# A block substitution in a two-layer mixer kernel: three runs of 128 blocks on GpSimd instead of four of 96 on two engines

## The chip, the core and the metric

The kernel runs on one core of a Trainium2 chip. The core has TensorE (PE, with its weight loads shown as PEld), VectorE (DVE), ScalarE (ACT), GpSimd (POOL) and SyncE (SP), which here issues every DMA. Each engine, and SP's queue of DMAs, executes its instructions in the order in which they stand in the program; between engines semaphores order the work. The metric is device time in microseconds (us) of one execution, as the median of several runs.

## The reference

Two blocks are computed one after the other for 512 tokens of width 2048, in fp32. The first has a state-space mixer (SSD) and a gated delta rule mixer (GDN) side by side, the second a layer with HGRN2 and an RG-LRU and a layer with an mLSTM. The change lies in the GDN of the first block: 8 heads, 2 directions, 6 chunks of 128 tokens (2 of context, 4 of latents). Cut to what matters:

```
gcum = cumsum(g);  decay = exp(where(incl, gcum[i] - gcum[j], -inf))
a_strict = where(strict, (k*beta) @ k.T * decay, 0)              # 128 x 128 for each head, direction, chunk
sol = triangular_solve(a_strict, rhs, left_side=True, lower=True, unit_diagonal=True)
u, w = sol[..., :V], sol[..., V:]
# then over the chunks:  v_new = u - w @ S;  o = q_dec @ S + attn @ v_new;  S = S*dec + k_end.T @ v_new
```

The kernel does the triangular solve by inverting (I + a_strict): first the 32 x 32 blocks on the diagonal, by substitution, and from these the inverse of 64 x 64 and of 128 x 128 with matmuls. There are 8 heads x 2 directions x 6 chunks x 4 blocks = 384 such 32 x 32 blocks.

## The kernel before

Every large matrix product multiplies fp32 weights that are split into a high and a low part of type fp32r. `gemm_steps` streams them: a DMA `wr` (L182) brings four blocks of 128 x 128, ScalarE copies them to `wh` (L185), VectorE makes the rest `wl` (L186), and TensorE does three products for each (L200). There are 4 buffers of `wr` and 6 of `wh` and `wl`.

**Phase A** (`phase_a`, some 0 to 705 us) projects and convolves. Its last part makes, head by head, what the recurrence needs: `gdn_prep(h)` loads `kf`, `vf`, and decay rows `E`; on GpSimd stand L677 (six subtractions on `E`), L703 (a square root of six columns, for which L702 on VectorE must be done) and L684 (a mask). It ends with L742, which stores the head's 48 diagonal blocks in DRAM, in `LX`. Between the heads stand the projections of the later heads' keys and values. In this phase a scheduler decides the order of all engines.

**The substitution** is `gdn_solve`: a DMA brings blocks from `LX`, one block per partition, into `T` (L751); GpSimd writes the diagonal (L753); then come 31 steps of a product (L758, `To<-T`) and a subtraction (L760, `T<-T,To`), 62 instructions of 31 to 256 elements per partition, each of which needs the one before it; GpSimd masks the result (L761) and writes the diagonal (L763), and a DMA stores it in `LT` (L764). It is called four times for two heads (96 blocks) each: twice in phase A with GpSimd as its engine, twice in phase B with VectorE.

**Phase B** (`phase_b`, some 700 to 1115 us) runs the recurrence of the 8 heads. `gdn_load(h)` (loads at L961: `X`, and `ZF`, `WB` from `LT`) and GpSimd's L902 and L905 prepare the inverse, `gdn_merge` builds it (matmuls `mg`, L928), `gdn_ctx` and `gdn_lat` walk over the chunks: `ks` (L975), `rS` on VectorE (L976), `vn` (L983), and so on. In `gdn_lat` the norm of q is made as `rq`: ScalarE writes it (L1033), GpSimd raises it in place to the power -1/2 (L1034), VectorE scales it in place (L1067); the scaled value is used only at the head's end (L1072). Between these small matmuls TensorE works through the projections of `z` and the later queries; `ssd_gate` adds up squares on GpSimd (L1190), and after four of them `ssd_norm` sums over partitions with the matmul `rs` (L294). In phase B TensorE's order is that of the code, written by hand (`weave`, `feed`); the scheduler orders the other engines and SP.

After it come the output projection, the gate and the second block; nothing there is touched.

Of the kernel before, what the change touches and what calls it, by code (L numbers as in the profile page):

```python
# [15 lines left out]
P = 128  # L16
# [117 lines left out]
class Prog:  # L134
# [606 lines left out]
                x = xt  # L741
            nc.sync.dma_start(self.LX[h, d].rearrange("c b r n -> (b r) c n"), x)  # L742

    def gdn_solve(self, h, g, eng):

        nc = self.nc
        n = 96
        flat = lambda t: t[h:h + 2].rearrange("a d c b r n -> (a d c b) (r n)")
        T = g.tile([n, 32, 32], F32, name="T", bufs=1)
        tf = T.rearrange("p r n -> p (r n)")  # L750
        nc.sync.dma_start(tf, flat(self.LX))  # L751

        nc.gpsimd.memset(tf[:, 0:1024:33], 2.0)  # L753
        t = g.tile([n, 256], F32, name="To", bufs=1)
        for j in range(31):
            a, b = 31 - j, j + 1
            o = t[:, :a * b].rearrange("p (a b) -> p a b", b=b)
            eng.tensor_tensor(out=o, in0=T[:, j + 1:, j:j + 1].to_broadcast([n, a, b]),  # L758
                              in1=T[:, j:j + 1, 0:b].to_broadcast([n, a, b]), op=MUL)
            eng.tensor_tensor(out=T[:, j + 1:, 0:b], in0=T[:, j + 1:, 0:b], in1=o, op=SUB)  # L760
        nc.gpsimd.affine_select(out=T, in_=T, pattern=[[1, 32], [-1, 32]], compare_op=ALU.is_gt, fill=0.0,  # L761
                                base=0, channel_multiplier=0)
        nc.gpsimd.memset(tf[:, 0:1024:33], 1.0)  # L763
        nc.sync.dma_start(flat(self.LT), tf)  # L764

    def phase_a(self):
        nc, tc, D = self.nc, self.tc, self.D
        d = self.dr
        dt = lambda n, s: d.tile(s, F32, name=n)
        self.yr = dt("yr", [8, P, 512])  # L770
        self.kD, self.vD = dt("kD", [8, P, 768]), dt("vD", [8, P, 768])
        self.ED = dt("ED", [8, 2, P, 512])
        self.ktD, self.vtD = dt("ktD", [8, P, 6, P]), dt("vtD", [8, P, 6, P])
        self.XD = dt("XD", [8, P, 768])
        self.LX, self.LT = dt("LX", [8, 2, 6, 4, 32, 32]), dt("LT", [8, 2, 6, 4, 32, 32])
        b1 = self.b1
        self.Dg = b1.tile([P, 8, 2, 6], F32, name="Dg")
        self.DDE = b1.tile([P, 8, 2, 6], F32, name="DDE")
        self.half6 = b1.tile([P, 6], F32, name="half6")
        nc.gpsimd.memset(self.half6, 0.5)  # L780

        xbc = D["w_xbc"]
        X, B, C = (lambda j: xbc[j]), (lambda g: xbc[8 + g]), (lambda g: xbc[10 + g])
        K, V = (lambda h: D["w_qkv"][8 + h]), (lambda h: D["w_qkv"][16 + h])
        self.xts = {}

        def sink_x(j):
            def f(lat, ctx):
                u = j // 2
                if j % 2 == 0:  # L790
                    self.xts[u] = self.sp.tile([P, 6, 256], F32, tag="xt", name="xt", bufs=2)
                o = (j % 2) * P
                self.to_tm(self.xts[u][:, :, o:o + P], lat, ctx)
            return f

        def sink_kv(dst, h):
            def f(lat, ctx):
                nc.sync.dma_start(dst[h, :, 256:768], lat)
                nc.sync.dma_start(dst[h, :, 0:256], ctx)
            return f  # L800

        cb = self.conv_block
        bx = lambda j, **k: self.both(X(j), cb("cs", j, True, sink_x(j)), **k)
        bB = lambda g, **k: self.both(B(g), cb("cs", 8 + g, True, lambda l, c: self.ssd_bc("B", l, c)), **k)

        def bC(g):
            taps = cb("cs", 10 + g, True, lambda l, c: self.ssd_bc("C", l, c))
            return self.lat(C(g), self.xh, self.xl, lambda ps: taps(ps))

        bk = lambda h: self.both(K(h), cb("cg", 8 + h, False, sink_kv(self.kD, h)))  # L810
        bv = lambda h: self.both(V(h), cb("cg", 16 + h, False, sink_kv(self.vD, h)))

        def small(ps, pc):
            self.small_done(ps[:96], pc[:96])
            self.sp = tc.alloc_tile_pool(name="sp", bufs=1, side="right")

        s0, s1 = self.pc.tile([P, 512], F32, tag="pc", name="s0"), self.pc.tile([P, 512], F32, tag="pc", name="s1")
        self.gemm([bB(0, share=(s0, 0)), bx(0, share=(s0, 256)), bx(1, share=(s1, 0)),
                   dict(self.both(D["w_small"], small, share=(s1, 256)), first=True)])
        self.pc.release()  # L820
        self.pq.release()
        self.pq = tc.alloc_tile_pool(name="pq", bufs=4, space=PSUM, reuse_waits="tile")
        self.gemm([bC(0)])
        self.ssd_cb()
        self.gemm([bx(2)])
        self.ssd_unit(0, self.xts[0])
        self.gemm([bx(3)])
        self.ssd_unit(1, self.xts[1])
        for h in (0, 1):
            self.gemm([bk(h)])  # L830
            self.gemm([bv(h)])
        self.gemm([bB(1)])
        self.gemm([bC(1)])
        self.ssd_cb()
        for u in (2, 3):
            for j in (2 * u, 2 * u + 1):
                self.gemm([bx(j)])
            self.ssd_unit(u, self.xts[u])
        self.sp.release()
        self.b2 = tc.alloc_tile_pool(name="b2", bufs=1, side="right")  # L840
        with tc.tile_pool(name="gp", bufs=1, side="right") as self.gp:
            self.gemm([bk(2)])
            self.gdn_prep(0)
            self.gemm([bv(2)])
            self.gdn_prep(1)
            self.gdn_solve(0, self.gp, nc.gpsimd)
            for h in range(2, 8):
                if h < 7:
                    self.gemm([bk(h + 1)])
                if h == 7:  # L850
                    self.qf = []
                    for _ in self.query(0):
                        pass
                self.gdn_prep(h)
                if h < 7:
                    self.gemm([bv(h + 1)])
                if h == 3:
                    self.gdn_solve(2, self.gp, nc.gpsimd)


            for _ in self.query(1):
                pass
            self.gemm([self.lat(D["w_z"][0], self.xh, self.xl, lambda ps: setattr(self, "z0", ps))])
# [221 lines left out]
    def phase_b(self):  # L1085
        nc, tc, D = self.nc, self.tc, self.D
        self.yF = self.dr.tile([16, P, 512], F32, name="yF")
        with (tc.tile_pool(name="cq", bufs=1) as self.cv, tc.tile_pool(name="gq", bufs=1, side="right", reuse_waits="tile") as g):
# [9 lines left out]
            for n in ("X32", "X64"):  # L1098
                t = g.tile([P, 6, P], F32, name=n)
# [49 lines left out]
            with tc.manual_schedule(engines={E.PE}):  # L1149

                wm = sum(FEED[n] for n in ("q1", "q2", "q3", "q4"))
                wc = FEED["ks"] + 2 * FEED["vn"] + 2 * FEED["sc"]
                wl = FEED["qk"] + 4 * (FEED["ks"] + FEED["vn"]) + 3 * FEED["so"]
                tail = FEED["x7"] / 10
                self.weave(others(), 21 * 48, FEED["f0"] + wm + wc + (7 + tail) * wl)
                with tc.manual_schedule(engines={E.SP}):
                    with tc.high_priority():
                        hd = self.gdn_load(0)
                        self.gdn_data(0, hd)
                    self.feed(FEED["f0"])  # L1160
                self.ssd_gate(0, self.zgate(self.z0, self.b2, tc.keep_in_program_order))
                self.run_slots(self.gdn_merge(hd))
                self.run_slots(self.gdn_ctx(0, hd))
                nx = self.gdn_load(1)
                for h in range(8):

                    pre = iter(())
                    if h < 7:
                        self.gdn_data(h + 1, nx)
                        pre = itertools.chain(self.gdn_merge(nx), self.gdn_ctx(h + 1, nx))  # L1170
                    o[h] = self.run_slots(self.gdn_lat(h, hd, self.qf[h], lambda: finish(h - 1) if h else None), pre, FEED["p0"], 1.0 if h < 7 else tail)
                    for _ in pre:
                        pass
                    hd, nx = nx, self.gdn_load(h + 2) if h < 6 else None
                    if h in (0, 2):
                        self.gdn_solve(4 + h, g, nc.vector)
                self.feed_all()

    def ssd_gate(self, h, z):
# [845 lines left out]
```

## Time and profile before

| | us |
|---|---|
| median of 3 runs | 3480.12 (3478.94 to 3483.15) |
| profiled execution, device time | 3485.06 |
| its span, first to last instruction | 3483.3 |
| TensorE busy in it | 3350.1 |
| VectorE, ScalarE, GpSimd busy | 2084.5, 1444.8, 412.4 |

The profile is of one execution. Its busy times are sums over the whole span; what an engine's instruction waited for is shown stage by stage, in the lists of waits and in the timelines, where a row gives the start, the duration, the engine, the line, the tiles and in brackets the idle time before it and what ended that. The granted clock of TensorE (PEclk) is a share of its full speed.

### The profile page before, as it was taken

The numbers are of one execution on the slowest core, as the hardware profiler recorded it, in microseconds if no ns is written. First come the engines' busy times: TensorE is split into PE (matmuls) and PEld (weight loads), VectorE is DVE, ScalarE is ACT, GpSimd is POOL, SyncE is SP. The second block draws the span as 40 slices with busy tenths as digits, with TensorE's granted clock in tenths as the row PEclk, the third lists the DMA queues.
The fourth block names the chain that finished last, engine by engine and source line by source line (L and its number), as shares of the span: only waits on it lengthen the run. The fifth ranks groups of instructions, "written<-read, shape, count | busy, mean of one in ns | idle before, by whom it ended". The sixth has DMA issues, their size and how long they took to land.

```text
span 3483.3 us, 48554 instructions
## 1 busy us (share of the span) xinstructions
PE 3350.1 (96%) x17334; PEld 2807.5 (81%) x17334; DVE 2084.5 (60%) x4129; ACT 1444.8 (41%) x2907; POOL 412.4 (12%) x596
## 2 busy tenths in 40 slices
PE   5999999889999999999999999999999999999998
PEld 4888888778888787778888788887888888888887
DVE  5678777778665648666656645455444444353446
ACT  4443434354444336654444445343333333342334
POOL 0011127721110001002222100000000000000000
PEclk8999999999999999999999999999999999999999
DMA  9533347555434854333333544543333333354345
GB/s 378 186 96 106 85 120 255 171 151 161 124 113 118 278 182 157 111 97 99 102 98 100 187 131 129 151 127 105 108 107 101 102 100 103 94 157 130 90 130 168
DMA packets 277121, 479.73 MB, mean 138 GB/s; under 512 B 51896, under 2 KB 85048, under 8 KB 272656
## 3 DMA queue, kind: packets, MB, share of 16 engines
q1 hardware_dynamic: 276880, 476.64, 45.4%
q8 instruction: 136, 2.23, 0.3%
q14 instruction: 105, 0.86, 0.1%
HBM read 415.17 MB, written 61.34 MB: 137 GB/s over the span
## 4 chain that ended last, share of the span: by engine, by line
PE 73%; DVE 10%; DMA 9%; ACT 3%; issue 3%; POOL 2%; SPq 0%; DVEq 0%; ACTq 0%; POOLq 0%
PE mm L200 54%; PE mm L228 3%; PE mm L229 3%; PE mm L230 3%; PE mmc L200 2%; DVE wl L186 2%; DMA wg<-in_wgate 1%; DMA araw<-yF 1%; PE pl L200 1%; PE mg L928 1%; PE pr L347 1%; ACT wh L185 1%; DMA wa<-in_wada 1%; DMA Rf<-AA 1%; PE s L200 1%
## 5 line engine op out<-in xcount | busy, mean ns | idle before, releaser
L200 PE MATMUL mm<-hi,wl 128*128 128x512 f32 (+2 forms) x3632 | 1415.9, 391 | 17.6 <-DVE wl L186 9.6
L200 PE MATMUL mm<-hi,wh 128*128 128x512 f32 (+2 forms) x3632 | 1417.7, 390 | 0.0
L200 PE MATMUL mm<-xlo,wh 128*128 128x512 f32 (+2 forms) x3632 | 1417.4, 390 | 0.4 <-DVE xlo L286 0.3
L185 ACT ACTIVATE wh<-wr 128x512 fp32r<-128x512 f32 (+1 forms) x940 | 581.2, 621 | 1120.5 <-PE mm L200 860.6
L186 DVE TENSOR_TENSOR wl<-wr,wh 128x512 fp32r<-128x512 f32 (+1 forms) x940 | 649.5, 696 | 659.5 <-ACT wh L185 655.9
L200 PEld LDWEIGHTS mm<-hi,wl 128*128 128x128 f32 (+1 forms) x3632 | 685.2, 189 | 144.4 <-DVE wl L186 14.6
L200 PEld LDWEIGHTS mm<-xlo,wh 128*128 128x128 f32 (+1 forms) x3632 | 685.3, 189 | 134.8 <-DVE xlo L286 2.9
L200 PEld LDWEIGHTS mm<-hi,wh 128*128 128x128 f32 (+1 forms) x3632 | 685.2, 189 | 119.5 <-issue 4.3
L228 PE MATMUL mm<-wl,hi 128*128 128x256 f32 (+1 forms) x512 | 173.4, 339 | 0.0
L229 PE MATMUL mm<-wh,xlo 128*128 128x256 f32 (+1 forms) x512 | 172.2, 336 | 0.0
L230 PE MATMUL mm<-wh,hi 128*128 128x256 f32 (+1 forms) x512 | 172.0, 336 | 0.0
L223 DVE TENSOR_TENSOR wl<-wr,wh 128x512 fp32r<-128x512 f32 x96 | 72.2, 753 | 90.2 <-ACT wh L222 89.6
L222 ACT ACTIVATE wh<-wr 128x512 fp32r<-128x512 f32 x96 | 60.5, 631 | 139.5 <-PE mm L230 71.8
L200 PE MATMUL mmc<-xlo,wh 128*128 128x256 f32 x368 | 106.3, 289 | 0.0
L200 PE MATMUL mmc<-hi,wl 128*128 128x256 f32 x368 | 105.7, 287 | 0.0
L228 PEld LDWEIGHTS mm<-wl,hi 128*128 128x128 f32 x512 | 97.1, 190 | 10.5 <-DVE pad L1357 0.3
L200 PE MATMUL mmc<-hi,wh 128*128 128x256 f32 x368 | 105.6, 287 | 0.0
L229 PEld LDWEIGHTS mm<-wh,xlo 128*128 128x128 f32 x512 | 97.1, 190 | 10.0
L230 PEld LDWEIGHTS mm<-wh,hi 128*128 128x128 f32 x512 | 97.1, 190 | 9.9
L442 DVE SCALAR_TENSOR_TENSOR cvl<-padl,hc,cvl 128x512 f32<-128x512 f32 x112 | 89.9, 809 | 24.1 <-ACT cvl L438 13.9
L200 PEld LDWEIGHTS mmc<-xlo,wh 128*128 128x128 f32 x368 | 69.9, 190 | 15.7
L200 PEld LDWEIGHTS mmc<-hi,wh 128*128 128x128 f32 x368 | 70.0, 190 | 15.0
(584 smaller groups left out, 3981.6 us busy)
## 6 DMA issues: line engine op xcount, KB each, us to landing
wr<-in_o_in SPq DMA_DIRECT2D x192, 256.0 KB, 3.0
wr<-in_e_in SPq DMA_DIRECT2D x160, 256.0 KB, 3.1
wr<-in_pgate SPq DMA_DIRECT2D x148, 256.0 KB, 3.3
wa<-in_wada SPq DMA_DIRECT2D x16, 2048.0 KB, 9.5
wr<-in_w_qkv SPq DMA_DIRECT2D x96, 256.0 KB, 3.2
wr<-in_w_z SPq DMA_DIRECT2D x64, 256.0 KB, 3.2
wr<-in_w_out SPq DMA_DIRECT2D x64, 256.0 KB, 4.5
wg<-in_wgate SPq DMA_DIRECT2D x16, 1024.0 KB, 7.6
```

Of the source, the lines that this page charges most:

```text
L185: nc.scalar.activation(out=hi, in_=r, func=AF.Copy)
L186: nc.vector.tensor_tensor(out=lo, in0=r, in1=hi.bitcast(F32), op=SUB)
L200: nc.tensor.matmul(ap, w[:, kk, :], x, start=(n == 0), stop=(n == total[key] - 1))
L222: nc.scalar.activation(out=hi, in_=r, func=AF.Copy)
L223: nc.vector.tensor_tensor(out=lo, in0=r, in1=hi.bitcast(F32), op=SUB)
L228: nc.tensor.matmul(ps[c][:, :n], self.xh[k][:, t], lo[:, i], start=first, stop=False)
L229: nc.tensor.matmul(ps[c][:, :n], self.xl[k][:, t], hi[:, i], start=False, stop=False)
L230: nc.tensor.matmul(ps[c][:, :n], self.xh[k][:, t], hi[:, i], start=False, stop=last)
L347: nc.tensor.matmul(pr[32 * j:32 * j + 32, 0:256], c32[:, 4 * q + j, :], w[:, 4 * q + j, :], start=(q == 0), stop=(q == 3), tile_position=( ...
L442: nc.vector.scalar_tensor_tensor(out=ov, in0=pad[:, :, j:j + n], scalar=taps[j], in1=ov, op0=MUL, op1=ADD)
L928: nc.tensor.matmul(v[:, c], lhs[:, c], rhs[:, c], start=True, stop=True)
```

## The change

`gdn_solve` now takes 128 blocks, one in each partition, as a flat third of `LX` and `LT` that does not end with a head: the first third is heads 0, 1 and 32 blocks of head 2, and so on. The first call stands behind `gdn_prep(2)`, the second behind `gdn_prep(5)`, the third in phase B behind head 0's recurrence, where one of VectorE's two stood; all three run on GpSimd. The line numbers move by one.

```diff
-    def gdn_solve(self, h, g, eng):
+    def gdn_solve(self, i, g, eng):
+
 
         nc = self.nc
-        n = 96
-        flat = lambda t: t[h:h + 2].rearrange("a d c b r n -> (a d c b) (r n)")
+        n = P
+        flat = lambda t: t.rearrange("a d c b r n -> (a d c b) (r n)")[P * i:P * i + P]
...
             self.gdn_prep(1)
-            self.gdn_solve(0, self.gp, nc.gpsimd)
             for h in range(2, 8):
...
-                if h == 3:
-                    self.gdn_solve(2, self.gp, nc.gpsimd)
+                if h in (2, 5):
+                    self.gdn_solve(h // 3, self.gp, nc.gpsimd)
...
                     hd, nx = nx, self.gdn_load(h + 2) if h < 6 else None
-                    if h in (0, 2):
-                        self.gdn_solve(4 + h, g, nc.vector)
+                    if h == 0:
+                        self.gdn_solve(2, g, nc.gpsimd)
```

The scheduler orders the instructions anew. TensorE's order in phase B is the same row for row; in phase A the transposes and products of `gdn_prep` move by up to some 28 matmuls. Three places follow.

SP's queue at the end of phase A, before. `LX<-Xs` and `LX<-Xt` store the last head's blocks; the branch ends the phase, and the loads of head 0 follow:

```order
L699 DMA ktD<-kt 128x768
L764 DMA LT<-T 96x1024
L715 DMA vtD<-vt 128x768
L685 DMA ED<-vf 128x512
L726 DMA XD<-X 128x768
L742 DMA LX<-Xs_7141 128x6x32
L742 DMA LX<-Xt 128x6x32
L1959 UNCONDITIONAL_BRANCH
L961 DMA X<-XD 128x768
```

The same place after:

```order
L699 DMA ktD<-kt 128x768
L715 DMA vtD<-vt 128x768
L685 DMA ED<-vf 128x512
L726 DMA XD<-X 128x768
L742 DMA LX<-Xs_7141 128x6x32
L742 DMA LX<-Xt 128x6x32
L765 DMA LT<-T 128x1024
L1959 UNCONDITIONAL_BRANCH
L961 DMA X<-XD 128x768
```

The store of the second substitution moved from before the last head's stores to behind all of them, directly ahead of phase B's first load; on GpSimd the last head's L703 and L684 moved into that substitution.

GpSimd in phase B while head 0's recurrence runs, before. `sqq` are the squares, `rq` is head 0's norm, `X_7335` and `X_7337` are the off-diagonal parts for the merge:

```order
L1190 TENSOR_TENSOR acc<-acc,sqq 128x512
L753 MEMSET T 96x32
L902 TENSOR_TENSOR X_7335<-X,Dg 32x6x32 x4
L905 TENSOR_TENSOR X_7337<-X,Dg 64x6x64 x2
L1190 TENSOR_TENSOR acc<-acc,sqq 128x512
L1034 TENSOR_TENSOR rq<-rq,mhalf 128x4
L1190 TENSOR_TENSOR acc<-acc,sqq 128x512
```

After, the stretch around L1034. Ahead of it, behind L754 (the old L753), stand 54 of the 62 instructions of the third substitution, with L902 and L905 behind the 11th and the second L1190 behind the 30th:

```order
L759 TENSOR_TENSOR To<-T 128x135
L761 TENSOR_TENSOR T<-T,To 128x5x27
L1034 TENSOR_TENSOR rq<-rq,mhalf 128x4
L759 TENSOR_TENSOR To<-T 128x112
L761 TENSOR_TENSOR T<-T,To 128x4x28
L759 TENSOR_TENSOR To<-T 128x87
L761 TENSOR_TENSOR T<-T,To 128x3x29
L759 TENSOR_TENSOR To<-T 128x60
L761 TENSOR_TENSOR T<-T,To 128x2x30
L759 TENSOR_TENSOR To<-T 128x31
L761 TENSOR_TENSOR T<-T,To 128x31
L762 AFFINE_SELECT T<-T 128x1024
```

L1034 and the third L1190, which were the first and second next things to do behind the second L1190, now have 24 instructions of the substitution ahead of them, the latter all of it.

VectorE at the same place, before; `wl` is a weight part, `Yf`, `El` and `rS` belong to head 0's recurrence:

```order
L1043 TENSOR_TENSOR Yf<-qk,Yf 128x512
L1043 TENSOR_TENSOR El<-qk,El 128x512
L186 TENSOR_TENSOR wl<-wr,wh 128x512
L1067 TENSOR_SCALAR rq<-rq 128x4
L760 TENSOR_TENSOR T<-T,To 96x18x14
L976 SCALAR_TENSOR_TENSOR rS<-ks,EAg,vt 128x128 x2
L1068 TENSOR_TENSOR tq<-rq 128x4
L758 TENSOR_TENSOR To<-T 96x255
```

And after:

```order
L1043 TENSOR_TENSOR Yf<-qk,Yf 128x512
L1043 TENSOR_TENSOR El<-qk,El 128x512
L186 TENSOR_TENSOR wl<-wr,wh 128x512
L1067 TENSOR_SCALAR rq<-rq 128x4
L1068 TENSOR_TENSOR tq<-rq 128x4
L976 SCALAR_TENSOR_TENSOR rS<-ks,EAg,vt 128x128 x2
L891 STREAM_TRANSPOSE ZB<-WB 128x192
L186 TENSOR_TENSOR wl<-wr,wh 128x512
```

The substitution's rows are gone from VectorE; L1067, which needs L1034, stands where it stood, two rows ahead of the pair `rS`.

In SP's queue of phase B the store of the third substitution (L765) stands behind the load of its `T` with head 1's `X` and `WB` and some loads of weights between, and more loads of weights and head 1's `ZF` stand behind the store.

## Rows read from the trace of the kernel before

**Rows 1.** The page's first part: busy us, share of span, instructions.

```profile
PE 3350.1 (96%) x17334; PEld 2807.5 (81%) x17334; DVE 2084.5 (60%) x4129; ACT 1444.8 (41%) x2907; POOL 412.4 (12%) x596
```

**Rows 2.** Waits of PE, 700 to 900 us: total, times, longest.

```profile
PE vn L983 <- DVE rC L976: 2.7, 2, 2.3
PE mg L928 <- DVE sso L1070: 2.1, 3, 1.3
...
PE vn L983 <- DVE rS L976: 1.1, 1, 1.1
PE sn L997 <- DVE veC L986: 1.0, 1, 1.0
```

**Rows 3.** Instruction groups: POOL 500 to 700 us, then DVE 690 to 900 us.

```profile
L760 POOL TENSOR_TENSOR T<-T,To 96x31 f32<-96x31 f32 (+15 forms) x62 | 43.4, 700 | 4.6
L758 POOL TENSOR_TENSOR To<-T 96x31 f32<-96x31 f32 (+15 forms) x62 | 40.1, 648 | 4.2
L684 POOL TENSOR_TENSOR vf<-E,mL 128x512 f32<-128x512 f32 x8 | 10.5, 1318 | 0.0
...
L760 DVE TENSOR_TENSOR T<-T,To 96x31 f32<-96x31 f32 (+15 forms) x62 | 25.0, 403 | 1.5
L758 DVE TENSOR_TENSOR To<-T 96x31 f32<-96x31 f32 (+15 forms) x62 | 24.0, 386 | 1.4
```

**Rows 4.** Windows, second substitution on POOL, lines L758 and L760 alone.

```profile
core 0: us, POOL busy (x), PEclk, DMA share, GB/s
634.10:640.82 6.72, 5.85 (x11) 1.00 0.64 198
640.83:657.92 17.09, 13.29 (x19) 0.70 0.39 117
657.93:681.82 23.89, 18.43 (x24) 1.00 0.51 151
681.83:687.30 5.47, 4.79 (x8) 1.00 0.44 133
```

**Rows 5.** Windows, all engines, inside the second substitution.

```profile
core 0: us, PE busy (x) PEld busy (x) DVE busy (x) ACT busy (x) POOL busy (x), PEclk, DMA share, GB/s
644.90:650.30 5.40, 4.93 (x18) 4.45 (x19) 0.02 (x1) 0.00 (x0) 4.85 (x8) 0.50 0.32 120
672.00:676.60 4.60, 4.60 (x22) 3.78 (x21) 4.60 (x6) 1.05 (x2) 4.25 (x5) 1.00 0.38 119
```

**Rows 6.** Timeline of POOL in phase A.

```profile
548.90 0.16 POOL L753 MEMSET T<- 96x32 f32 x1 [0.19 <-DMA T<-LX]
...
571.14 1.29 POOL L684 TENSOR_TENSOR vf<-E,mL 128x512 f32<-128x512 f32 x1
...
623.85 0.16 POOL L763 MEMSET T<- 96x32 f32 x1
...
633.92 0.15 POOL L753 MEMSET T<- 96x32 f32 x1 [9.35 <-DMA T<-LX]
...
688.97 0.15 POOL L763 MEMSET T<- 96x32 f32 x1
689.31 1.35 POOL L703 TENSOR_TENSOR ss<-ss,half 128x6 f32<-128x6 f32 x1 [0.19 <-DVE rk L702]
```

**Rows 7.** Timeline at the phases' boundary: SP's queue, then PE.

```profile
695.99 0.56 SPq L961 DMA_DIRECT2D X<-XD  x1
...
699.20 3.17 SPq L182 DMA_DIRECT2D wr<-in_w_z  x4
...
707.46 0.50 PE L200 MATMUL mm<-hi,wl 128*128 128x512 f32 x1 [1.97 <-DVE wl L186]
```

**Rows 8.** Timeline of POOL in phase B.

```profile
736.60 0.15 POOL L753 MEMSET T<- 96x32 f32 x1 [7.20 <-DMA T<-LX]
738.26 2.86 POOL L902 TENSOR_TENSOR X<-X,Dg 32x192 f32<-32x192 f32 x4 [1.51 <-DMA X<-XD]
741.20 1.73 POOL L905 TENSOR_TENSOR X<-X,Dg 64x384 f32<-64x384 f32 x2
747.62 1.28 POOL L1190 TENSOR_TENSOR acc<-acc,sqq 128x512 f32<-128x512 f32 x1 [4.69 <-ACT sqq L1189]
756.13 1.03 POOL L1034 TENSOR_TENSOR rq<-rq,mhalf 128x4 f32<-128x4 f32 x1 [7.23 <-ACT rq L1033]
```

**Rows 9.** Timeline of DVE, then PE, in phase B.

```profile
757.45 0.16 DVE L1067 TENSOR_SCALAR rq<-rq 128x4 f32<-128x4 f32 x1
...
757.93 0.61 DVE L976 SCALAR_TENSOR_TENSOR rS<-ks,EAg,vt 128x128 f32<-128x128 f32 x2
...
761.13 0.61 PE L983 MATMUL vn<-rS,W 128*128 128x128 f32 x4
...
773.28 1.02 PE L294 MATMUL rs<-acc,ones 128*128 128x512 f32 x2
```

**Rows 10.** PE around its longest wait in phase A; then a window.

```profile
645.37 1.54 PE L312 MATMUL vT<-ident,vf 128*128 128x128 f32 x6 [7.53 <-DMA vf<-vD]
...
645.40:651.00 5.60, 5.60 (x21) 5.02 (x22) 0.00 (x0) 0.00 (x0) 5.05 (x9) 0.50 0.22 85
```

## The prediction

> **What bounds the kernel now.** The page's first part comes first: TensorE is busy for 3350.1 of 3483.3 us [rows 1], and it takes its instructions in order, so the time changes only where the change lengthens or shortens a wait of TensorE. I then read the list of TensorE's waits from 700 to 900 us, the stretch in which VectorE does its two substitutions [rows 2]: the largest is 2.7 us, and those on VectorE that the substitutions could have caused (rC, sso, rS, veC) come to 6.9 us. That is the ceiling of what freeing VectorE can give there. Third come the groups of the substitution itself: two on GpSimd take 43.4 + 40.1 us, two on VectorE 25.0 + 24.0 us [rows 3]. GpSimd has room (412.4 us busy of 3483.3). So the question is not busy time but what now stands behind a long chain on an engine that works in order, and who waits for it. For that I read the orders of GpSimd, VectorE and SP against the timeline of before.
>
> **The price of one substitution.** On VectorE one costs (25.0 + 24.0)/2 = 24.5 us. On GpSimd the windows show the second one cut into its first 11, next 19, next 24 and last 8 instructions [rows 4]: 6.7 us, 17.1 us less 2.6 for an L684 and an L703 that stand between (durations 1.3 and 1.35 [rows 3, 6]) = 14.5 us, 23.9 us less some 3.7 for a head's six L677 = 20.2 us, and 5.5 us, together 46.9 us with the gaps. That 128 partitions are used for 96 should cost nothing: L684 does 512 elements in each of 128 partitions in 1.32 us [rows 3], 2.6 ns for an element of a partition, and the eight substitution instructions in the window with an idle VectorE, of 207 to 240 elements, take 4.85/8 = 0.61 us on 96 partitions [rows 5], about 2.7 ns. I take the same price for both widths; were it in proportion to the partitions, a third more, each term below would grow by a third.
>
> **Phase A: the boundary moves.** The first substitution now starts behind head 3's L684, which ended at 572.4 [rows 6]; since no substitution stands before it and its transposes come 18 to 28 short matmuls earlier, I estimate 570.5. Before, the first took from 548.9 to 624.0, 75.1 us, with other work of GpSimd between. Of that, head 2's L684 and head 3's L677, L703 and L684 are now ahead of it (1.3 + 3.9 + 1.35 + 1.3 = 7.9 us), which leaves 67.2, less some 1 to 3 us of waits for loads that now come in time: 66. It ends at 636.5. From its end to the start of the next, before, went 633.92 - 624.0 = 9.9 us (store, load of the next T): 646.5. The second took 633.9 to 689.1 = 55.2 us, and now has the last head's L703 and L684 inside, 2.7 us more: 646.5 + 57.9 = 704.4. A bound from below is that same L703, which waited for VectorE until 689.3 [rows 6]; behind it stand 16 instructions (some 10 us), L684 and the mask, so no end before some 699 unless TensorE is far ahead. The store follows at once, and directly behind it in SP's queue is phase B's first load, which went out at 695.99 [rows 7]. It moves to about 704.7, by 8.7 us; the bounds are 3 (699) and 12 (each substitution a tenth longer in GpSimd's mixed company). I take 8. TensorE used up its weights at 705.5 and went on at 707.46, when the weights issued from 699.20 on had been split [rows 7]; those loads stand behind the first load in the same queue, so TensorE goes on at about 715.5. What TensorE may gain in phase A by shorter waits is swallowed here, since this end is set by GpSimd and SP. **Term 1: +8 us.**
>
> **Phase B: VectorE waits for GpSimd.** L1067 on VectorE needs L1034 on GpSimd. Before, L1034 ended at 757.16 and L1067 ran at 757.45, unhindered [rows 8, 9]. Now 54 of the substitution's 62 instructions stand ahead of L1034. In the times of before: T is there at 736.6, with a third more bytes say 737.0; + 0.2 for the diagonal; + 6.7 for 11 instructions; + 2.86 + 1.73 for L902 and L905 [rows 8] = 748.5; + 14.5 for 19 = 763.0; + 1.3 for L1190 = 764.3, long after its input is ready; + 24 instructions; + 1.0 for L1034. For the 24 there are two prices. Rows 4 give 20.2 us. But from 757.5 on VectorE stands still, and with an idle VectorE eight instructions took 4.85 us busy, 0.69 us each with the gap, against 4.25/5 + 0.08 = 0.93 us with a VectorE that was busy throughout [rows 5]. 24 x 0.69 = 16.6 us; I take 17. The Trainium skill (SBUF — State Buffer, Who interferes with whom) says that a VectorE instruction with two SBUF inputs and a GpSimd instruction that reads SBUF exclude each other, the later one blocking fully; by that rule the 24 run alone and the shorter price holds, without it the sum would be 3 us higher. The two windows agree with it. L1034 is done at 782.3. VectorE then does L1067, L1068 and the pair rS, 0.9 us: 783.2. TensorE wants rS for vn, which it began at 761.13 without a wait [rows 9]; its order there has not changed. So TensorE stands for 783.2 - 761.1 = 22 us, 26 with the longer price, and 18 if T lands 4 us sooner because the DMAs are less crowded (it had taken 9 us from issue). I take 23. **Term 2: +23 us.** It adds to term 1, because SP's loads, T among them, move with the boundary.
>
> **The clock.** After TensorE's wait of 7.53 us at 637.8 the granted clock was 0.50, its lower level of 1.2 GHz, for 5.6 us, in which half the work was done [rows 10]: 2.8 us lost. The same follows twice now; the first loss is partly swallowed by the wait of term 2, of the second nothing. **Term 3: +4 us** (1 to 5.6).
>
> **VectorE relieved.** 124 instructions, 49 us, leave VectorE. Up to 6.9 us of TensorE's waits [rows 2] could go, but rC and veC lie ahead of the new wait and are swallowed by it, and sso recurs in heads without a substitution. **Term 4: -2 us** (0 to -5).
>
> **What I cost at nothing, and its cover.** The store L765 in phase B blocks SP until the substitution ends, some 789; loads of weights stand behind it. Cover: up to 4 raw and 6 split buffers, of 12 matmuls each, and TensorE stands still until 783 itself. The third L1190 and rs: TensorE comes to rs 12.15 us after vn [rows 9], 795; GpSimd has finished the last 8 instructions, the mask (1.3) and that L1190 by 791. The margin is 4 us; whatever GpSimd is slower beyond it is paid. X for the merge is 5 us later and was 15 us early.
>
> **Sum.** 8 + 23 + 4 - 2 = +33 us. The profiled execution has 3483.3 us of span and 1.8 around it, 5 us over the median; by the sum its like would be 3518 us, and against the median of the runs 3480.1 + 33 = 3513 us.
>
> **The rivals.** (a) Only VectorE's wait: GpSimd's second substitution ends in phase A in time, for instance because its instructions run at the pace of an idle VectorE there too. For it: 62 x 0.69 = 43 us would be 4 us less in each substitution. Against it: VectorE was busy in most of that stretch, and the last head's L703 binds. Term 1 falls to 0 and its clock loss too: 23 + 2.8 - 2 = +24, 3504 us. (b) All that and a second wait, at rs or for weights behind L765: GpSimd slower than taken, by a third in proportion to partitions or by VectorE catching up. A third on 46.9 us is 15 us in each: terms 1 and 2 become 30 and 38, some +70, 3550 us; a mild form with a wait of 5 to 10 us gives 3520 to 3525. Against: the rows on partitions above. (c) The other side, faster: the new wait does not bind TensorE and the relief of VectorE decides, up to 6.9 us: 3473 us. It decides only if L1034 ends by some 761, within 24 us of T's landing, when 54 instructions, L902, L905 and L1190 stand before it; GpSimd would need half the time that any row shows. (d) The change does not do what it says: the wait is not there because VectorE passes L1067 by. It works in order, and rS stands behind L1067 in its order; the boundary alone would give +8, 3488 us.
>
> **How the numbers follow.** Forecast 0.74, (a) 0.13, (b) 0.08, (c) 0.03, (d) 0.02. The forecast's own bounds: 3 + 18 + 1 - 5 = +17 at the low end, 12 + 26 + 5.6 = +44 at the high end. The range, 3497 to 3526, takes in most of these, all of (a) and the mild form of (b). A measurement here tells 0.2% (7 us) from no change; (d) lies just above that, and I split it. So faster 0.03, same 0.03, slower 0.94.
>
> **What would show it.** In the profile after: a wait of TensorE at vn (L983) for rS of about 22 us, some 760 to 795 us into the span; VectorE idle before L1067 for some 25 us, ended by GpSimd's L1034; GpSimd without a gap from T's diagonal to L1034; TensorE at 0.50 for some 5 us behind it. At the boundary, SP's L765 directly ahead of X<-XD, both near 704, and TensorE waiting for wl for some 10 us. From 900 us on every row is shifted by one constant. It is wrong if VectorE's wait at L1067 is under 10 us, if substitution instructions on 128 partitions are slower than on 96, or if the time after 1200 us changes.

## The result, and the profile after

The changed kernel takes 3508.64 us (median of 4 runs, 3501.45 to 3510.98), the kernel before, beside it, 3481.64 us. The ratio is 1.0072, with a 95% interval of 1.0057 to 1.0088: slower by some 25 us (20 to 31). The forecast was 3513, +33. One execution of all that follow, the profiled one of st_only, ran at a granted clock of 0.653 and took 4790 us; it is left out.

The profiled execution has a span of 3507.9 us, 24.6 more than before. The page's first part of it (busy us, share of span, instructions) answers to [rows 1]: TensorE is as busy as before, VectorE does 43 us less, GpSimd 31 us more.

```profile
PE 3352.8 (96%) x17334; PEld 2813.9 (80%) x17334; DVE 2041.9 (58%) x4005; ACT 1445.5 (41%) x2907; POOL 443.8 (13%) x655
```

The waits of TensorE (total, times, longest), first from 700 to 760 us, then from 760 to 800, answer to [rows 2] and to the wait in [rows 7]:

```profile
PE mm L200 <- DVE wl L186: 8.4, 1, 8.4
...
PE vn L983 <- DVE rS L976: 24.2, 1, 24.2
```

The second is the forecast's new wait, where the list of before had no single wait over 2.3 us (its 2.7 is the sum of two). Its chain stands in the timelines. GpSimd in phase B, from T's diagonal to L1034 (the first and the last of the 24 instructions that stand directly ahead of L1034, and L1034):

```profile
738.66 0.16 POOL L754 MEMSET T<- 128x32 f32 x1 [5.96 <-DMA T<-LX]
...
764.57 0.64 POOL L759 TENSOR_TENSOR To<-T 128x256 f32<-128x256 f32 x1
...
779.95 0.45 POOL L761 TENSOR_TENSOR T<-T,To 128x135 f32<-128x135 f32 x1
780.35 1.03 POOL L1034 TENSOR_TENSOR rq<-rq,mhalf 128x4 f32<-128x4 f32 x1
```

VectorE, then TensorE, behind it, against 757.45, 761.13 and 773.28 in [rows 9]:

```profile
781.42 0.34 DVE L1067 TENSOR_SCALAR rq<-rq 128x4 f32<-128x4 f32 x1 [27.14 <-POOL rq L1034]
781.80 0.16 DVE L1068 TENSOR_TENSOR tq<-rq 128x4 f32<-128x4 f32 x1
781.88 0.60 DVE L976 SCALAR_TENSOR_TENSOR rS<-ks,EAg,vt 128x128 f32<-128x128 f32 x2
```

```profile
782.28 1.22 PE L983 MATMUL vn<-rS,W 128*128 128x128 f32 x4 [24.25 <-DVE rS L976]
...
797.80 1.02 PE L294 MATMUL rs<-acc,ones 128*128 128x512 f32 x2
```

VectorE stands 27.14 us with the two instructions for `rS` ready behind L1067, because L1067 needs a value of 128 x 4 elements that GpSimd makes behind 54 instructions of the substitution.

The boundary between the phases, SP's queue and then TensorE, answers to [rows 7]:

```profile
700.02 0.33 SPq L765 DMA_DIRECT2D LT<-T  x1
700.40 0.43 SPq L961 DMA_DIRECT2D X<-XD  x1
```

```profile
711.27 0.80 PE L200 MATMUL mm<-hi,wl 128*128 128x512 f32 x1 [8.42 <-DVE wl L186]
```

The first load goes out 4.4 us later than before, TensorE goes on 3.8 us later. What the two waits cost behind themselves is in the windows of TensorE (busy, granted clock, DMA):

```profile
711.20:714.00 2.80, 2.73 (x7) 0.50 0.58 196
...
782.20:789.30 7.10, 7.02 (x25) 0.50 0.28 87
```

At 0.50, the level of 1.2 GHz, half of these 9.9 us is lost: 5.0 us. From there on the two executions run alike to within 2 us. The last vn of phase B starts at 1115.3 in before and 1138.5 in after, 23.2 us later, and the span's end is 24.6 us later. The 23.2 is the better figure: from the last vn to the end, where no version here changes anything, the profiles take 2362 to 2371 us, so spans of single executions can differ by some us for no reason that lies in the change.

### The profile page after: what moved, and what is told of

Its sections match the earlier page's. It is cut to its first block, busy times and chain, and to the rows that moved or that the text cites. A ratio compares the mean times of both kernels' runs of the same rounds, so it can differ in the third digit from the quotient of the medians.

```text
span 3507.9 us, 48480 instructions
## 1 busy us (share of the span) xinstructions
PE 3352.8 (96%) x17334; PEld 2813.9 (80%) x17334; DVE 2041.9 (58%) x4005; ACT 1445.5 (41%) x2907; POOL 443.8 (13%) x655
## 4 chain that ended last, share of the span: by engine, by line
PE 79%; DVE 8%; DMA 5%; POOL 4%; ACT 2%; issue 2%; SPq 0%; DVEq 0%; POOLq 0%; ACTq 0%
PE mm L200 58%; PE mm L228 3%; PE mm L229 3%; PE mm L230 3%; PE mmc L200 2%; DVE wl L186 1%; PE mg L928 1%; PE pl L200 1%; POOL T L761 1%; POOL To L759 1%; DMA E<-AA 1%; PE pr L347 1%; PE s L200 1%; DMA araw<-yF 1%; POOL E L677 1%
## 5 line engine op out<-in xcount | busy, mean ns | idle before, releaser
L185 ACT ACTIVATE wh<-wr 128x512 fp32r<-128x512 f32 (+1 forms) x940 | 581.1, 621 | 1127.5 <-PE mm L200 876.3
```

The source lines that it names most:

```text
L185: nc.scalar.activation(out=hi, in_=r, func=AF.Copy)
```

## The experiments

All are timed against the kernel before on the same chip; differences in us are the ratio of that comparison times 3480.

**rq_pool: take L1067 away from VectorE.**

```diff
-        nc.vector.tensor_scalar(out=rq, in0=rq, scalar1=float(P) ** -0.5, scalar2=None, op0=MUL)
-        nc.vector.tensor_tensor(out=t, in0=rq, in1=rq, op=MUL)
+        nc.gpsimd.tensor_scalar(out=rq, in0=rq, scalar1=float(P) ** -0.5, scalar2=None, op0=MUL)
+        nc.gpsimd.tensor_tensor(out=t, in0=rq, in1=rq, op=MUL)
```

> The changed kernel with L1067 and L1068 (the two small scalings of rq, all heads) moved from VectorE to GpSimd, right behind L1034, so that VectorE's order holds nothing that waits for L1034; nothing else is touched. Theory: the 24.2 us that TensorE waits at vn (L983) in the changed kernel are VectorE standing at L1067; they vanish, but the third L1190 still stands behind the whole third substitution, which now runs beside a working VectorE and ends some 3 us later, at about 790. TensorE reaches rs (L294), which needs that L1190, at about 770 and waits there until about 791, some 20 us. So the wait moves by 12 us of work and the time falls by 0 to 5 us only: about 3505 us, 23 us over the kernel before. Rival 1: VectorE's wait was all there is; then the time falls by 24 us and some 3 of the clock, to about 3482. Rival 2: it was not L1067 that held VectorE; then vn waits as before and the time stays at 3508.

Measured: 3506.73 us, ratio 1.0073 (1.0060 to 1.0086), no less than the change itself. TensorE's and GpSimd's timelines show why:

```profile
759.34 0.61 PE L983 MATMUL vn<-rS,W 128*128 128x128 f32 x4
...
789.72 2.08 PE L294 MATMUL rs<-acc,ones 128*128 128x512 f32 x2 [12.27 <-POOL acc L1190]
```

```profile
788.41 1.26 POOL L1190 TENSOR_TENSOR acc<-acc,sqq 128x512 f32<-128x512 f32 x1
```

vn no longer waits, so it was L1067 that held VectorE. But TensorE now waits at rs for the third L1190, which stands behind the whole substitution. That wait is 12.3 us and not the 20 expected, with shorter ones (3.2 at `og`, 2.3 at vn) beside it; rs itself starts 8 us ahead of the changed kernel's, and by the last vn of phase B (1137.2) that lead has shrunk to 1.3.

**rq_sq: take L1190 away from GpSimd too.** Beside the edit of rq_pool:

```diff
-            nc.gpsimd.tensor_tensor(out=self.ssq, in0=self.ssq, in1=sq, op=ADD)
+            nc.vector.tensor_tensor(out=self.ssq, in0=self.ssq, in1=sq, op=ADD)
```

> As rq_pool, and the adding up of squares (L1190, six instructions in all) moved to VectorE too, so that neither vn nor rs hangs on GpSimd's substitution. Theory: both waits vanish; what is left of the change is the later boundary between the phases (TensorE goes on 3.8 us later in the changed kernel, and about 2 us more at the lower clock) and VectorE's relief (some 5 us in the other direction). So about 3481 us, within 4 us of the kernel before. The substitution's last 24 instructions take 20 us beside a working VectorE, where they took 17 beside a standing one. If SP, which stands at the store of the substitution (L765) until some 790, starves TensorE, a wait for wl of 3 to 8 us shows near 790 and the time is 3485 to 3489. Rival: GpSimd's substitution slows VectorE itself by sharing SBUF with it; then VectorE's instructions between 740 and 790 are longer and the time stays above 3490.

Measured: 3504.51 us, ratio 1.0062 (1.0048 to 1.0075). The expectation failed, and so did the rival's reason. A wait of 20 us is there again, at the second vn of head 0's latent chunks. VectorE, SP's queue and TensorE:

```profile
796.76 0.38 DVE L892 STREAM_TRANSPOSE WF<-ZF 128x192 f32<-128x192 f32 x1 [25.46 <-DMA ZF<-LT]
```

```profile
758.40 0.33 SPq L182 DMA_DIRECT2D wr<-in_w_qkv  x1
790.79 0.33 SPq L765 DMA_DIRECT2D LT<-T  x1
791.21 0.38 SPq L182 DMA_DIRECT2D wr<-in_w_qkv  x1
791.68 0.75 SPq L961 DMA_DIRECT2D ZF<-LT  x1
```

```profile
797.43 1.22 PE L983 MATMUL vn<-rS,W 128*128 128x128 f32 x4 [20.00 <-DVE rS L976]
```

SP issues nothing for 32 us, because the store of the substitution is next in its queue. The weights behind it have cover; the small load of `ZF` has none: VectorE's L892 waits for it, and `rS` stands behind L892. In the changed kernel the same load went out at 789.31 and was hidden behind the wait at L1067.

**rq_sq_st: take the store out of SP's queue too,** for the third substitution. Beside the edits of rq_sq:

```diff
-        nc.sync.dma_start(flat(self.LT), tf)
+        (nc.gpsimd if i == 2 else nc.sync).dma_start(flat(self.LT), tf)
```

> As rq_sq (L1067, L1068 on GpSimd, L1190 on VectorE), and the store of the third substitution (L765) is issued from GpSimd's own queue and no longer from SP's. In rq_sq TensorE still waited 20.0 us at vn, for VectorE at L892, which waited 25.5 us for the load of ZF, which stood in SP's queue behind that store. Theory: three things of phase B stand behind GpSimd's third substitution (L1067 on VectorE, L1190 on GpSimd, the loads behind L765 in SP's queue), each enough for some 20 us and each hiding the next; with all three taken away no wait over 3 us is left from 760 to 800 us, and the time is that of the kernel before, plus some 4 us of the boundary (third_vec), less 2 to 7 us of VectorE's relief: 3474 to 3484 us. Rival: a fourth thing waits, or GpSimd's DMA issue is itself slow; then a wait of TensorE of 10 us and more stands in that stretch and the time stays above 3490.

Measured: 3485.47 us, ratio 1.0008 (1.0000 to 1.0017), 3 us over the kernel before. The waits of TensorE from 760 to 800 us are now:

```profile
PE og L1052 <- ACT o L1055: 1.7, 1, 1.7
PE og L1053 <- ACT vn L990: 1.3, 1, 1.3
PE mg L928 <- DVE W L931: 0.9, 1, 0.9
PE vn L983 <- DVE rS L976: 0.5, 1, 0.5
```

Three things stood behind GpSimd's substitution, and each hid the next: of the versions run (L1067 moved; L1067 and L1190 moved; the store alone moved; all three) only the last is faster, by some 20 us. The store with just one of the two moves was not run.

**st_only: the store alone.** The last edit without the others.

> The changed kernel with only the store of the third substitution (L765) issued from GpSimd's queue; L1067 and L1190 as in the changed kernel. Theory of three waits that hide each other: the first, VectorE at L1067, stays, so vn waits some 24 us and the time stays at about 3508 us, within 4 us of the changed kernel. Rival: the blocked SP queue is what costs; then the time falls by 20 us to some 3487.

Measured: 3509.02 us (median of five, 3505 to 3514), ratio 1.0079 (1.0064 to 1.0094). As expected, nothing is gained. That L1067 still holds VectorE is inferred from this; no row of st_only is shown for it.

**before_edits: the control.** The two moves of rq_sq in the kernel before.

> The kernel before with the two moves that rq_sq made (L1067 and L1068 on GpSimd, L1190 on VectorE) and no change of the substitution. This is the control: what these moves cost by themselves. Theory: six additions of 0.7 us more on VectorE and eight short pairs of instructions on GpSimd are hidden; the time stays within 3 us of the kernel before, 3480 to 3483. Rival: they cost 5 us and more, and the boundary's and the waits' shares read from rq_sq and rq_sq_st have to be reduced by that.

Measured: 3479.64 us, ratio 0.9993 (0.9984 to 1.0002). The moves cost nothing that can be seen, so the differences above belong to the waits.

**before_no_vec: VectorE's relief by itself.**

```diff
-        for j in range(31):
+        for j in range(31 if eng is nc.gpsimd else 0):
```

> The kernel before with the 2 x 62 products and subtractions of VectorE's two substitutions left out (the blocks of heads 4 to 7 are loaded, masked and stored unsolved); everything else stands. This measures what VectorE's relief is worth by itself, which the prediction took as 2 us, with 6.9 us as the ceiling. Theory: TensorE's waits for rC, veC, vn of head 0 (some 5 us from 730 to 750) go and the time falls by 4 to 7 us, to about 3475. Rival: those waits have other causes than the substitution; then the time stays within 2 us of 3480.

Measured: 3470.89 us, ratio 0.9970 (0.9958 to 0.9982), 10 us less (6 to 15), more than the 4 to 7 expected. In the profile the stretch from TensorE's resumption at the boundary to the last vn of phase B takes 398.5 us (708.17 to 1106.7), in the kernel before 407.8 (707.46 to 1115.3): 9.3 us. The waits from 705 to 760 us that are left:

```profile
PE vn L983 <- DVE W L931: 1.5, 2, 1.3
PE mm L200 <- DVE wl L186: 1.4, 1, 1.4
```

Against [rows 2], the waits for rC and veC are gone, and with them the dip of the clock that followed them in the kernel before (TensorE alone; busy, clock, DMA):

```profile
746.20:750.00 3.80, 3.36 (x10) 0.57 0.29 71
```

That is 1.6 us more. A second dip of the kernel before, 0.60 for the 3.4 us from 937.2 on, costs 1.4 us; without VectorE's work the granted clock is 1.00 from 705 to 1116 us. Summed over all of TensorE's listed waits from 705 to 1116 us, 21.7 us became 16.8. The 4.9 and the two dips make 7.9 of the 9.3 us; where the other 1.4 lie is open.

**third_vec: the third substitution on VectorE,** `self.gdn_solve(2, g, nc.vector)`.

> The changed kernel with the third substitution (128 blocks, phase B) on VectorE; the two in phase A stay as changed. Theory: this leaves the boundary alone: the first load of phase B goes out at about 700.4 for 696.0, TensorE goes on 3.8 us later and loses some 2 us at the lower clock; one VectorE substitution of 24.5 us is gone, which gives back 0 to 3 us. About +4 us on the kernel before (+1 to +7): 3485 us. If 128 partitions cost more than 96 on VectorE, its instructions are longer than 0.39 and 0.40 us on the mean. Rival: the boundary costs nothing that reaches the end, and the time is that of the kernel before or less.

Measured: 3484.30 us, ratio 1.0015 (1.0006 to 1.0024), 5 us (2 to 8), as expected. TensorE resumes at the boundary even later than in the changed kernel's profile:

```profile
715.75 0.79 PE L200 MATMUL mm<-hi,wl 128*128 128x512 f32 x1 [10.12 <-DVE wl L186]
```

This point scatters. Five profiles have phase A in the changed kernel's order, row for row on every engine (after, rq_pool, rq_sq, rq_sq_st, third_vec): 711.27, 712.37, 713.98, 714.52, 715.75, on the mean 713.6. Four have that of the kernel before (before, before_no_vec, before_edits, one_and_one_g): 707.46, 708.17, 703.84, 707.41, on the mean 706.7. The boundary costs 6.9 us by these, with a scatter of some 2 us in each group. The wait itself is clearer: 8.4 to 10.2 us in the five, 1.2 to 2.0 in the four. On VectorE the 31 subtractions and 31 products of 128 partitions take 437 and 388 ns on the mean here (400 and 375 in vec_early, below), against 403 and 386 for 96 in [rows 3].

**two_T and all_st: is it the store that moves the boundary?** In two_T the second substitution's blocks have a buffer of their own; in all_st, on top of rq_sq_st, all three stores are issued by GpSimd.

```diff
-        T = g.tile([n, 32, 32], F32, name="T", bufs=1)
+        T = g.tile([n, 32, 32], F32, name="T", bufs=2 if i < 2 else 1)
```

```diff
-        nc.sync.dma_start(flat(self.LT), tf)
+        nc.gpsimd.dma_start(flat(self.LT), tf)
```

> The changed kernel with two buffers for T in phase A, so that the second substitution's blocks are loaded while the first still runs, and its store (L765) stands ahead of the last head's stores in SP's queue. Theory: the second substitution starts at about 637 for 642.8 and ends by some 694 to 699; phase B's first load goes out at about 696 or earlier, TensorE goes on at about 707.5 for 711.3, and the wait at vn stays at some 24 us. So 4 to 6 us less than the changed kernel: about 3503 us. Rival: the boundary's delay was swallowed by the wait at vn behind it, since GpSimd's third substitution starts from its own load; then the time stays at 3508.

> As rq_sq_st, with all three stores (L765) on GpSimd's queue, so that nothing stands between the last head's stores and phase B's first load in SP's queue. Theory: that load goes out at 693 to 698 us for 700.4 in the changed kernel, TensorE goes on at 706 to 709 for 711.3, and the time is 2 to 4 us under that of rq_sq_st: about 3475 us, 0 to 8 us under the kernel before. Rival: TensorE's arrival at the boundary sets the time, not the loads; then it is that of rq_sq_st.

Measured: two_T 3506.79 us, ratio 1.0069 (1.0057 to 1.0082); all_st 3486.91 us, ratio 1.0012 (1.0002 to 1.0021). Neither gain can be seen. (In both, some rows of phase A also stand in another order than in the changed kernel.) In two_T the boundary did move, to 709.02, and the first wait shrank to 2.7 us, but the time says nothing of it within its interval. all_st shows that the store was not the only thing that mattered. Without it SP's first load goes out at 699.81, 8.7 us before TensorE runs out of weights at 708.5 (2.5 us before in the changed kernel, 9.5 in the kernel before), and still TensorE waits 9.3 us and resumes at 717.81. ScalarE and GpSimd there:

```profile
711.59 0.36 ACT L908 ACTIVATE t<-ZF 32x192 f32<-32x192 f32 x1 [8.25 <-POOL mhalf L1105]
```

```profile
707.07 0.16 POOL L764 MEMSET T<- 128x32 f32 x1
...
711.47 0.13 POOL L1105 MEMSET mhalf<- 128x4 f32 x1
```

Phase B's first memsets on GpSimd stand behind the substitution as well; ScalarE's L908 waits for them, and ScalarE's splits of the weights (L185) stand behind L908. One more thing hung on the same engine, hidden behind the store.

**no_second: the second substitution without its work.**

```diff
-        for j in range(31):
+        for j in range(31 if i != 1 else 0):
```

> The changed kernel with the 62 products and subtractions of the second substitution left out (blocks 128 to 255 are loaded, masked and stored unsolved); the first and the third stand as changed. This takes away what moved the boundary between the phases: GpSimd is free there, SP's queue is not held by L765, phase B's memsets on GpSimd are not behind a substitution. Theory: TensorE goes on after the boundary at some 707 to 708 us as in the kernel before (the changed phase A gave 711.3 to 715.8 in five profiles, 713.6 on the mean), the wait of some 24 us at vn stays: 4 to 7 us less than the changed kernel, about 3503 us. Rival: phase A's new order makes the boundary late by itself (transposes that wait for vf); then the resumption stays at 712 or later and the time at 3508.

Measured: 3492.38 us, ratio 1.0029 (1.0018 to 1.0041), 15 us under the changed kernel, at least twice the expected 4 to 7. TensorE at the boundary, GpSimd a little ahead, and TensorE's wait in phase B:

```profile
697.31 0.50 PE L200 MATMUL mm<-hi,wl 128*128 128x512 f32 x1 [0.57 <-DVE wl L186]
```

```profile
678.49 1.35 POOL L703 TENSOR_TENSOR ss<-ss,half 128x6 f32<-128x6 f32 x1 [18.30 <-DVE rk L702]
```

```profile
PE vn L983 <- DVE rS L976: 23.8, 1, 23.8
```

The boundary lies 14 us ahead of the changed kernel's and 10 ahead of that of the kernel before. So a substitution on GpSimd late in phase A is not free there in the changed kernel, where the preparation of the last heads shares GpSimd with it; for the kernel before this is inferred, as no run leaves out its second substitution alone. TensorE's waits for `vf` at vT from 560 to 700 us are 12.5 us in the changed kernel, 5.8 without the work. And the wait at vn stays the same, 23.8 us, 14 us sooner: the terms add, as the prediction said.

**one_and_one_g: a version meant to beat both.** The kernel before, with only the first of VectorE's two substitutions on GpSimd and the three waits taken away:

```diff
-                        self.gdn_solve(4 + h, g, nc.vector)
+                        self.gdn_solve(4 + h, g, nc.vector if h else nc.gpsimd)
```

> The kernel before's four substitutions of 96 blocks, phase A untouched; of the two in phase B the first runs on GpSimd with the three waits taken away as in rq_sq_st (L1067, L1068 on GpSimd, L1190 on VectorE, its store on GpSimd's queue), the second stays on VectorE, its T loaded from GpSimd's queue. Theory: no boundary cost, and the relief of the first VectorE substitution, which before_no_vec shows as some 6 of 9 us: 3474 us, 4 to 8 us under the kernel before. Rival: the one buffer of T makes the second wait for the first's store (7.4 us to landing in rq_sq_st), and GpSimd's memset of its diagonal holds X of head 2 (L902) or VectorE; then a wait of 5 to 15 us at mg or vn stands near 810 us and the time is 3480 to 3490.

Measured: 3502.22 us, ratio 1.0054 (1.0041 to 1.0066). The rival, but at another row, and beyond its 3490 us:

```profile
791.91 0.20 DVE L758 TENSOR_TENSOR To<-T 96x31 f32<-96x31 f32 x1 [29.25 <-POOL T L753]
```

The scheduler put the first instruction of VectorE's own substitution early in VectorE's queue; its T is the same buffer, free only when GpSimd's substitution is stored. VectorE stands 29.25 us and TensorE 21.6.

**vec_early: three of 128, placed otherwise.** GpSimd keeps the first only; the second is called with `nc.vector` ahead of `nx = self.gdn_load(1)`, the third with `nc.vector` behind head 2.

> Three substitutions of 128 blocks, placed otherwise than in the change: the first on GpSimd behind head 2's preparation, as changed; the second on VectorE in phase B, behind head 0's context steps; the third on VectorE behind head 2's recurrence. GpSimd's place in the last part of phase A is left free, which in no_second brought TensorE past the boundary at 697.3 us, 10 us ahead of the kernel before, and nothing in phase B hangs on a substitution of GpSimd's. Theory: the boundary at about 697 to 700 us, VectorE's two substitutions of 24.5 us cost what they cost in the kernel before, no wait over 3 us at vn: 8 to 10 us under the kernel before, about 3472 us. Rival: VectorE has no room so early in phase B (wl, W and rC wait for it) or SP stands at the store ahead of head 2's WB; then waits of 3 us and more at vn or mg stand from 730 to 800 us and the time is 3476 to 3485.

Measured: 3479.16 us, ratio 0.9987 (0.9978 to 0.9996): 29 us under the changed kernel and 4.5 us (1 to 8) under the kernel before, half of what was expected, and less than the 0.2% that the prediction took as the least that can be told from no change. No wait at vn or mg is over 1.6 us, so the rival's waits are not there either. TensorE resumes at 701.00; from there to the last vn it takes 409.6 us, 1.8 more than before. It is the only version here whose interval lies below the kernel before with nothing left out.

## Why the prediction came out as it did

The range (3497 to 3526) holds the time, and the main mechanism is the one in the trace. The point forecast does not hold as well: +33 lies above the interval of the measured difference (20 to 31). Two of the four terms were too large, and one cause was incomplete. By the times at which rows start, the boundary is later by 3.8 us, vn by another 17.3, and the last vn of phase B by another 2.0, in which the clock and VectorE's relief stand together: 23.2 in all, against 8 + 23 + (4 - 2) = 33. In this profile terms 1 and 2 missed by some 4 and 6 us, both the same way.

- **VectorE's wait, term 2, +23:** the mechanism is right, 27.14 us at L1067, ended by L1034, and the term is too large. The 24.2 us at vn must not be set against the 23, which was counted from 761.13, where vn began before. TensorE now comes to vn at 758.0, 46.8 us behind the boundary against 53.7 before, since VectorE no longer holds it up (47.2 in before_no_vec), and stands the longer for it. Counted as the prediction did, vn begins 21.15 us later (782.28), 3.8 of them the boundary's, which leaves 17.3 (17.6 in two_T and in no_second). The working had 22.1 and rounded up. T landed 2.1 us later than before (738.66 for 736.60), where the working had the boundary's shift and 0.4 us for more bytes. And from there to the end of L1034 the working had 45.3 us (737.0 to 782.3); it took 42.7 (738.66 to 781.38). The choice between two prices for the 24 instructions was right: 764.57 to 780.40 is 15.8 us, 0.66 each, against the 17 taken and 20.2 by [rows 4]. In rq_sq_st, where VectorE is busy for 10.3 us beside them, the same 24 take 16.9 us (768.03 to 784.93), so at this place the choice was worth 1.1 us and not 3. Where the two engines meet, GpSimd, then VectorE:

```profile
767.27 0.68 POOL L761 TENSOR_TENSOR T<-T,To 128x255 f32<-128x255 f32 x1
768.03 0.65 POOL L759 TENSOR_TENSOR To<-T 128x256 f32<-128x256 f32 x1
768.76 1.05 POOL L761 TENSOR_TENSOR T<-T,To 128x256 f32<-128x256 f32 x1
```

```profile
767.34 0.74 DVE L931 TENSOR_SCALAR W<-mg 32x192 f32<-32x192 f32 x2
768.11 1.11 DVE L1190 TENSOR_TENSOR acc<-acc,sqq 128x512 f32<-128x512 f32 x1
```

Beside L931, whose one input `mg` is not in SBUF, L761 takes 0.68. L759 began 0.08 us ahead of L1190, which has two inputs in SBUF, and keeps its 0.65 us (0.64 in the changed kernel); L1190, the later, takes 1.11 against a median of 0.69 in this run, and the L761 that begins while L1190 runs takes 1.05 against 0.73. This is the pair of instructions that the rule cited in the prediction names (the Trainium skill, SBUF — State Buffer, Who interferes with whom). By the rule the later one blocks fully. The rows agree that the later one is held; full blocking would give an estimated 1.26 and 1.19 us (what is left of the earlier one, and then its own time), and they took some 0.15 less.

- **128 partitions at the price of 96:** right. On GpSimd the groups of the changed kernel, 500 to 800 us, against 700 and 648 ns in [rows 3]:

```profile
L761 POOL TENSOR_TENSOR T<-T,To 128x31 f32<-128x31 f32 (+15 forms) x93 | 60.4, 649 | 6.8
L759 POOL TENSOR_TENSOR To<-T 128x31 f32<-128x31 f32 (+15 forms) x93 | 57.3, 617 | 6.6
```

The third substitution among them ran in part beside a VectorE that stood still. Like with like, the two of phase A alone, 500 to 702 us, give:

```profile
L761 POOL TENSOR_TENSOR T<-T,To 128x31 f32<-128x31 f32 (+15 forms) x62 | 41.6, 671 | 4.4
L759 POOL TENSOR_TENSOR To<-T 128x31 f32<-128x31 f32 (+15 forms) x62 | 41.2, 664 | 4.3
```

- **The boundary, term 1, +8:** 3.8 us in the profile, 6.9 by the means of nine. The substitution ended at 700.0, near the lower bound of 699, for 704.4: the first ended at 636.6, as forecast, but the second's blocks landed 6.2 us later and not 9.9. The means come near the 8; the reason given, a store directly ahead of the first load, was one of at least two things that hang there (all_st). And the lower bound was not one: L703, which [rows 6] showed waiting for VectorE until 689.3, ran at 686.32 in the changed kernel and at 678.49 in no_second. Much of that wait was itself an effect of the substitution's work on GpSimd.
- **The clock, term 3, +4:** 5.0 us, of the size forecast; the first 1.4 of them lie ahead of vn and are swallowed by its wait. The dips further on cannot be settled from single profiles: the changed kernel's has three more of 3.4 us (at 830.6, 960.4 and 1004.7), the kernel before's one (937.2), that of rq_sq_st none behind 795.
- **VectorE relieved, term 4, -2:** the "ceiling" of 6.9 was not one: the relief is worth 9 to 10 us (before_no_vec). It counted four kinds of wait in one window of before, and left out waits for W and the clock behind the waits. In the changed kernel most of the relief lies ahead of vn, where the wait swallows it, as the prediction said; what is left is, with the clock, in the 2.0 above, against 4 - 2. So the term is small for the reason given; how much of the 2.0 is relief is not shown.
- **What was costed at nothing:** in the changed kernel it did cost nothing, but because TensorE stood still anyway. With that wait gone, the third L1190 costs 12 us (rq_pool) and the store in SP's queue 20 us (rq_sq). For the store the prediction named the weights and their cover and overlooked `ZF`.
- **The rivals:** (a), VectorE's wait alone, gave +24, nearer to the measured 25 than the forecast, and the time alone would favour it. The boundary excludes it: TensorE waits there 8.4 to 10.2 us in five profiles, 1.2 to 2.0 in four, and no_second gives back 15 us. (b), a second wait or a slower GpSimd, falls: there is no wait at rs or for wl from 760 to 800 us, and 128 partitions cost what 96 do. (In its sum the two substitutions of phase A at 15 us each would make term 1 some 38, not 30.) (c), faster, falls: L1034 ended 20 us too late for it. So does (d): VectorE did not pass L1067.

## What to carry to other kernels

A long chain that is moved to an idle engine is paid for by every small instruction that the order leaves behind it, and by every queue in which its store stands; list them all, because each such wait hides the next, and removing one or two shows nothing (rq_pool, st_only, rq_sq) until the last is gone (rq_sq_st). What the relieved engine gives back is best measured by leaving its work out: a list of waits for it undercounted it here (6.9 against 9.3 us). And a row of the trace that waits for another engine is a lower bound only if that engine was not itself held up by the work in question.

## What the hardware showed that was not expected

- One and the same GpSimd subtraction, 256 elements in each of 128 partitions, took 0.73 us in the changed kernel while VectorE stood still, and 1.05 in rq_sq_st beside VectorE's L1190; so the price of a chain on GpSimd depends on what VectorE does beside it (15.8 and 16.9 us for the 24 instructions):

```profile
765.29 0.73 POOL L761 TENSOR_TENSOR T<-T,To 128x256 f32<-128x256 f32 x1
```

- The time from first load to TensorE's resumption at the boundary is steady (10.9 to 11.7 us in twelve profiles; only in all_st, where something else held it, 18.0), but the boundary itself moves by 4 us between executions of the same order, as much as term 1 read from two single profiles.
